# Paged latent decode woven into a feed-forward: six steps per half, three key buffers, scores in three bursts

## The chip, the cores and the metric

The kernel runs on one core of a Trainium2 chip. The metric is the device time of one execution in microseconds; three executions of the kernel before gave 1323.63, 1324.40 and 1324.49 us, median 1324.4. The engines are named as in the profile: PE is TensorE (PEld its weight loads), DVE VectorE, ACT ScalarE, POOL GpSimd, SP the queue that issues most DMAs.

## The reference

One layer of a hybrid decoder for 512 prompt tokens and a sample group of 8 sequences with 4 new tokens each, all in f32:

```python
h = x + 0.5 * post1(SwiGLU_1(pre1(x)))
u = pre_mix(h); z = u @ w_in
# HGRN2 group, 4 heads: gated linear recurrence over z
# MLA group, 4 heads: latent softmax attention, latent 256 + rotary key 64
h = h + post_mix(concat(o_hgrn, o_mla) @ w_out)
y = h + 0.5 * post2(SwiGLU_2(pre2(h)))
```

The prompt attends to itself. Each sample sequence attends to 4096 past positions too, whose latent rows (256) and rotary keys (64) lie in a pool of pages of 128 rows, found through `page_table`:

```python
s = einsum('bqhr,bsr->bhqs', ql, c_kv) + einsum('bqhd,bsd->bhqs', qr, k_rope)
p = softmax(where(k_pos <= q_pos, s * scale, -inf))
o_lat = einsum('bhqs,bsr->bqhr', p, c_kv)
```

## The kernel before, in words

**Tokens and products.** The 544 tokens are kept transposed (features on the partitions) in two halves: x = 0 holds 256 prompt tokens, x = 1 the other 256 and the 32 sample tokens (288 columns). Every large product is done in three passes of f32r: each operand is split into a rounded high piece and a remainder, and hi*hi, hi*lo and lo*hi are added up. A weight of 128 output columns (`weight`, L219) is loaded by SP into a raw buffer (`wraw`, 5 of them, L226), cast on ScalarE into `wh` (L237), and VectorE writes the remainder `wl` (L238). `wh` and `wl` have 2 buffers each, and 2 more while the second feed-forward's scope is open. `gemm` runs the 24 products of one weight and one half of the tokens.

**Stages.** First feed-forward for both halves (to 421 us), the mixer with the recurrence and the attention of the prompt (to 744 us), then the *decode stage*: the second feed-forward of half x = 0 (`gb`, an `ffn` generator, L297) is woven with the paged attention of the sample tokens. After it come the mixer's output projection for x = 1 with what is left of `gb` (`fill`, `FILL`), and the second feed-forward for x = 1.

**The feed-forward as a generator.** `ffn` walks the 22 column blocks of the inner width in four chunks of 6, 6, 5 and 5. For each block j it multiplies gate and up (48 products for one half of the tokens), forms the gated value and splits it into `hh` and `hl`, and yields. Behind each chunk it multiplies 8 down columns d (3 products for each inner block of the chunk) and yields after each. In all 54 such steps.

**The decode.** The 4096 x 8 past rows are 16 *halves* n (two for each sequence), each of two key blocks g of 128 partitions with 8 rows on each. A `Half` has these parts:
- `gather` (L1078): four indirect DMAs from POOL, two of latent rows (`craw`, 1 MB each, in six slots: three halves) and two of rotary keys (`rraw`, 4 buffers).
- `turn` (L1097): VectorE transposes both blocks in 32 x 32 squares into key buffers `kh` (`KHB` = 2 of them, so those of one half), six instructions at L1102 and L1103.
- `score` (L1106): 80 small f32 matmuls on 64 x 32 pieces of the array, two instructions each in the trace (160 records), for 10 key pieces j; after j = 9 VectorE takes the maxima.
- `peak` (L1126): TensorE turns the maxima, VectorE reduces them; `weigh` (L1135): two exponentials on ScalarE; `place` (L1140): VectorE transposes the weights into `pt`, then 16 small copies into `pbuf` (L1146), 8 on ScalarE and 8 on VectorE.
- `value` (L1148): 16 matmuls (32 records, L1154) of `pbuf` with the latent rows, which frees their slots; `gathered` (L1160) adds up every other half.

**The order around the change.** `decode` (L1168) runs three ticks for each half: in tick 0 the first five score pieces of half n - 2, a yield, then the other five, the values of n - 3 and the gather of n, a yield; in tick 1 the peak of n - 2 and the whole turn of n - 1, a yield; in tick 2 gathered(n - 3) and weigh(n - 2), a yield, place(n - 2). So four yields for a half. The driver below it (L1243 to L1254) takes 79 decode steps and 43 steps of `gb` in even proportion, and a step of a short generator for the new tokens with each decode step. Each engine works through its queue in order; the order in the queues follows the code, but the compiler's scheduler moves single instructions past one another.

Of the kernel before, what the change touches and what calls it, by code (L numbers as in the profile page):

```python
# [53 lines left out]
FILL = (4, (7, 8, 9), (1, 2, 3, 4), 4)  # L54
# [5 lines left out]
DRATE = 0.8  # L60
KHB = 2
# [42 lines left out]
def hybrid_step_kernel(  # L104
# [114 lines left out]
    def weight(srcs, kt, staged=False, home=None):  # L219
        if home is None and staged:  # L220
            pool, sfx, bufs = st, "x", STAG
        elif wx and wcnt[0] % (NW + WX) >= NW:
            pool, sfx, bufs = wx[0], "", WX
        else:
            pool, sfx, bufs = sb, "", NW
        w = mk([P, 8, P], F32, "wraw", 5, pool=sb)  # L226
        if home is None:
            wh = mk([P, 8, P], F32R, "wh" + sfx, bufs, pool=pool)
            wl = mk([P, 8, P], F32R, "wl" + sfx, bufs, pool=pool)
            wcnt[0] += not staged  # L230
# [25 lines left out]
    def gemm_q(wt, act_):  # L256
        wh, wl, kt = wt
        acc = ps("acc", "acc")
        n = act_[0].shape[-1]
        for k in range(kt):  # L260
            if k and k % 2 == 0:
                yield
            for i, (a, b) in enumerate(((wh, act_[0]), (wh, act_[1]), (wl, act_[0]))):
                nc.tensor.matmul(acc[:, :n], a[:, k], b[:, k], start=k + i == 0, stop=k == kt - 1 and i == 2)  # L264
        return acc[:, :n]

# [30 lines left out]
    def ffn(i, n_post, xs, u, nxt=None, mid=None, late=None, fin=None, pre=()):  # L297
# [5 lines left out]
        for c, (f0, nf) in enumerate(FCH[i]):  # L303
            hh = {x: mk([P, FCH[i][0][1], HS[x]], F32R, "hh" + "ab"[x], pool=pool) for x in xs}
            hl = {x: mk([P, FCH[i][0][1], HS[x]], F32R, "hl" + "ab"[x], pool=pool) for x in xs}
            for j in range(nf):
                f = f0 + j
                wg_ = (w0 or [weight([wcols(w_g[i], 0, KD, f * P)], KD)]).pop(0)
                ga = {x: gemm(wg_, u[x]) for x in xs}
# [3 lines left out]
                up = {x: gemm(wu_, u[x]) for x in xs}  # L313
# [16 lines left out]
            for grp in groups:  # L330
                wts = {d: pre.pop(0) if pre else weight([wcols(w_d[i], f0, nf, d * P)], nf, len(grp) > 1) for d in grp}
                for x in xs:
                    for d in grp:
                        acc = gemm(wts[d], (hh[x], hl[x]))
# [15 lines left out]
                yield  # L350
# [665 lines left out]
    gb = ffn(1, 5, (0,), u4, late=lambda: rstd_u(u4[0], 0), pre=seam)  # L1016
    next(gb)

    with scope("dec"):
# [48 lines left out]
        NS = 3 * NH2 + 11  # L1068
# [3 lines left out]
        class Half:  # L1072
# [24 lines left out]
            def turn(self):  # L1097
                self.kh = []
                for g in range(2):
                    kh = mk([P, ROWS, 10, 32], F32, "kh", KHB)  # L1100
                    for a in range(0, ROWS, 4):
                        nc.vector.transpose(kh[:, a : a + 4, :8].rearrange("p a j k -> p a (j k)"), self.craw[g][:, a : a + 4])  # L1102
                    nc.vector.transpose(kh[:, :, 8:].rearrange("p a j k -> p a (j k)"), self.rraw[g])  # L1103
                    self.kh.append(kh)
# [63 lines left out]
        def decode():  # L1168
            H = {}
            for t in range(NS):  # L1170
                n, r = divmod(t, 3)
# [4 lines left out]
                if n < NH2 and r == 0:  # L1176
                    H[n] = Half(n)
                if r == 0:
                    if at(2):
                        at(2).score(range(5))  # L1180
                    if n < 3 and at(0):
                        at(0).gather()
                    yield
                    if at(2):
                        at(2).score(range(5, 10))
                    if at(3):
                        at(3).value(H.get(n - 4))
                    if n >= 3 and at(0):
                        at(0).gather()
                    yield  # L1190
                elif r == 1:
                    if at(2):
                        at(2).peak()
                    if at(1):
                        at(1).turn()
                    yield
                else:
                    if at(3):
                        at(3).gathered()
                    if at(2):  # L1200
                        at(2).weigh()
                    yield
                    if at(2):
                        at(2).place()
# [39 lines left out]
        next(ga)  # L1244
        na, nb = NS + (NS + 2) // 3, int((22 + 32) * DRATE)
        ia, ib = 1, 0
        while ia < na:
            if ia * nb <= ib * na:
                next(ga, None)
                next(gn, None)  # L1250
                ia += 1
            else:
                next(gb, None)
# [165 lines left out]
```

## Time and profile before

| | us |
|---|---|
| median of three runs | 1324.4 |
| the profiled execution | 1323.85 |
| its span (first to last instruction) | 1322.1 |
| TensorE busy, granted clock | 1282.5, 0.995 |
| VectorE / ScalarE / GpSimd busy | 888.4 / 697.2 / 75.2 |

Busy time of TensorE counts a matmul from its start to a modelled end, and matmuls overlap in the pipeline; so its busy time is not useful time, and holes are read from the starts of neighbouring instructions. [...] "issue" as a releaser means that the profile shows nothing that the engine waited for.

### The profile page before, as it was taken

To read this page: it belongs to the slowest core of one execution; us is meant where nothing else is said; L and a number is where in the kernel's file an instruction comes from. 1 tells how busy PE (TensorE), PEld (TensorE's weight loads), DVE (VectorE), ACT (ScalarE), POOL (GpSimd) and SP (SyncE) were. 2 spreads that over 40 slices of the span, in tenths; PEclk is the share of its full clock that TensorE was granted. 3 is DMA by queue.
4 is the path that set the end of the run, shared out by engine and by line. 5 is a ranking of instruction groups with operands and counts; after the bars stand their busy time and mean duration, and the time that the engine had idled before them with its cause. 6 is when DMAs were issued, how large, how long until landed. Compare 5 with 4: busy or idle time off the path is not lost.

```text
span 1322.1 us, 30477 instructions
## 1 busy us (share of the span) xinstructions
PE 1282.5 (97%) x12696; PEld 1202.2 (91%) x12696; DVE 888.4 (67%) x1782; ACT 697.2 (53%) x1454; POOL 75.2 (6%) x79
## 2 busy tenths in 40 slices
PE   7999999999999999999999999989899999999997
PEld 7999999999999988889897887887788999999996
DVE  7553244434457787876867889989888868466664
ACT  6543344324456654444747665563455777554454
POOL 0000000000000000000000312313210000000000
PEclk9999999999999999999999999999899999999999
DMA  7323232333253323323222778968768645656551
GB/s 214 90 80 96 81 97 75 86 96 89 79 160 105 104 58 85 94 79 105 83 92 81 285 230 281 307 224 303 262 208 275 176 128 175 175 146 184 141 157 48
DMA packets 280552, 192.87 MB, mean 146 GB/s; under 512 B 12765, under 2 KB 271422, under 8 KB 275550
## 3 DMA queue, kind: packets, MB, share of 16 engines
q1 hardware_dynamic: 271968, 147.85, 38.8%
q0 software_dynamic: 7168, 41.95, 8.4%
q8 instruction: 100, 1.64, 0.5%
q10 hardware_dynamic: 1278, 1.12, 0.3%
q14 instruction: 38, 0.31, 0.1%
HBM read 181.22 MB, written 9.67 MB: 144 GB/s over the span
## 4 chain that ended last, share of the span: by engine, by line
PE 79%; DVE 11%; ACT 5%; issue 3%; DMA 2%; SPq 0%; DVEq 0%; ACTq 0%
PE acc L246 59%; PE acc L264 9%; DVE kh L1102 3%; DVE wl L238 2%; PE s L1115 2%; ACT wh L237 2%; PE s L919 1%; PE o L1154 1%; PE pa L658 1%; DMA wraw<-w_d 1%; PE zx L551 1%; ACT pbuf L1146 1%; DVE ssq L173 1%; PE pr L179 1%; DMA xt<-x_p 1%
## 5 line engine op out<-in xcount | busy, mean ns | idle before, releaser
L237 ACT CAST wh<-wraw 128x1024 fp32r<-128x1024 f32 (+3 forms) x255 | 248.2, 976 | 315.4 <-PE acc L246 276.6
L238 DVE TENSOR_TENSOR wl<-wraw,wh 128x1024 fp32r<-128x1024 f32 (+3 forms) x255 | 288.7, 1133 | 139.7 <-ACT wh L237 138.9
L246 PE MATMUL acc<-uhb,wh 128*128 128x288 f32 x768 | 227.9, 297 | 0.8 <-ACT uhb L195 0.8
L246 PE MATMUL acc<-ulb,wh 128*128 128x288 f32 x768 | 227.3, 296 | 0.0
L246 PE MATMUL acc<-uhb,wl 128*128 128x288 f32 x768 | 225.9, 295 | 1.2 <-DVE wl L238 1.2
L246 PE MATMUL acc<-uha,wh 128*128 128x256 f32 x768 | 220.3, 287 | 2.3 <-DVE sil L318 1.0
L246 PE MATMUL acc<-uha,wl 128*128 128x256 f32 x768 | 217.1, 284 | 1.3 <-DVE wl L238 1.2
L246 PE MATMUL acc<-ula,wh 128*128 128x256 f32 x768 | 217.1, 283 | 0.6 <-DVE ula L196 0.6
L246 PEld LDWEIGHTS acc<-uha,wh 128*128 128x128 f32 x768 | 145.5, 190 | 7.1 <-issue 3.3
L246 PEld LDWEIGHTS acc<-uha,wl 128*128 128x128 f32 x768 | 145.2, 190 | 2.3 <-DVE wl L238 2.3
L246 PEld LDWEIGHTS acc<-ula,wh 128*128 128x128 f32 x768 | 145.3, 189 | 1.1 <-DVE ula L196 1.0
L246 PEld LDWEIGHTS acc<-uhb,wl 128*128 128x128 f32 x768 | 144.5, 188 | 1.7 <-DVE wl L238 1.7
L246 PEld LDWEIGHTS acc<-uhb,wh 128*128 128x128 f32 x768 | 144.2, 188 | 1.6 <-ACT uhb L195 1.0
L246 PEld LDWEIGHTS acc<-ulb,wh 128*128 128x128 f32 x768 | 144.2, 188 | 0.1
L246 PE MATMUL acc<-hhb,wh 128*128 128x288 f32 x317 | 93.6, 297 | 0.9 <-ACT hhb L158 0.9
L246 PE MATMUL acc<-hlb,wh 128*128 128x288 f32 x317 | 94.0, 297 | 0.1
L246 PE MATMUL acc<-hhb,wl 128*128 128x288 f32 x317 | 93.0, 294 | 0.0
L246 PE MATMUL acc<-hha,wh 128*128 128x256 f32 x297 | 87.1, 293 | 1.4 <-ACT hha L158 1.4
L246 PE MATMUL acc<-hla,wh 128*128 128x256 f32 x297 | 84.4, 284 | 1.1 <-DVE hla L159 1.1
L246 PE MATMUL acc<-hha,wl 128*128 128x256 f32 x297 | 84.4, 284 | 0.3 <-DVE wl L238 0.2
L321 DVE TENSOR_TENSOR sil<-sil,acc 128x256 f32<-128x256 f32 (+1 forms) x88 | 38.2, 436 | 49.6 <-PE acc L246 47.7
L320 DVE TENSOR_TENSOR sil<-sil,sit 128x256 f32<-128x256 f32 (+1 forms) x88 | 38.5, 441 | 44.9 <-ACT sit L295 44.5
(476 smaller groups left out, 2765.7 us busy)
## 6 DMA issues: line engine op xcount, KB each, us to landing
wraw<-w_g SPq DMA_DIRECT2D x66, 512.0 KB, 4.3
wraw<-w_u SPq DMA_DIRECT2D x66, 512.0 KB, 4.0
wraw<-w_in SPq DMA_DIRECT2D x24, 512.0 KB, 4.0
wraw<-w_d SPq DMA_DIRECT2D x32, 384.0 KB, 4.3
wraw<-w_d SPq DMA_DIRECT2D x32, 320.0 KB, 3.3
wraw<-w_o SPq DMA_DIRECT2D x16, 512.0 KB, 4.1
wraw<-w_d SPq DMA_DIRECT2D x16, 448.0 KB, 3.7
wraw<-w_d SPq DMA_DIRECT2D x8, 512.0 KB, 4.0
```

The source lines that it names most:

```text
L173: (eng or nc.vector).tensor_tensor(acc, acc, q, op=ALU.add)
L179: nc.tensor.matmul(pr[:, :n], ones, acc, start=True, stop=True)
L237: nc.scalar.copy(wh[:, :kt], w[:, :kt])
L238: nc.vector.tensor_tensor(wl[:, :kt], w[:, :kt], f32(wh[:, :kt]), op=ALU.subtract)
L246: nc.tensor.matmul(out, a, b, start=n == 0, stop=n == last)
L264: nc.tensor.matmul(acc[:, :n], a[:, k], b[:, k], start=k + i == 0, stop=k == kt - 1 and i == 2)
L320: nc.vector.tensor_tensor(s, s, t, op=ALU.mult)
L321: nc.vector.tensor_tensor(s, s, up[x], op=ALU.mult)
L551: nc.tensor.matmul(z, w[a][:, k], U[1][b][:, k], start=k + n == 0, stop=k == KD - 1 and n == 2)
L658: nc.tensor.matmul(pa[es, c * 32 : (c + 1) * 32].rearrange("p (n m) -> p n m", m=m), kx[:, cs], up(qx[:, cs]), start=True, stop=True, skip ...
L1102: nc.vector.transpose(kh[:, a : a + 4, :8].rearrange("p a j k -> p a (j k)"), self.craw[g][:, a : a + 4])
L1115: nc.tensor.matmul(self.s[r][c * 32 : c * 32 + 32, :P], q[rs, j], kh, start=j == 0, stop=j == 9, skip_group_check=True)
```

## The change

- Scores in three bursts of 3, 3 and 4 key pieces, a yield after the first and the second. With the second burst the first key block of half n - 1 is turned (`turn(0)`); after the third burst the second block (`turn(1)`), then the values of n - 3 and the gather of n, a yield. Then peak, a yield; gathered and weigh, a yield; place runs together with the next first burst. Six yields ("steps") for a half, 114 in all. Key buffers `KHB` 2 to 3.
- The 16 placing copies are all on ScalarE.
- The feed-forward of x = 0 gets `fine=True`: gate and up products are cut in two pieces of 12 products with a yield between (`gemm_q` with step 4), and behind each chunk but the last the first two down columns are run together by `gemm_2`: all inner blocks but the last for both, a yield, then the last block for both. This makes 120 steps of what were 54.
- The driver takes one decode step, then `gb` steps in the proportion 100 to 114; the generator for the new tokens steps with every other decode step. `FILL[0]` goes from 4 to 13, since a step is now smaller: 100 steps end at the same inner block as 43 did.
- To make room, raw weight buffers go from 5 to 4 for the whole kernel, and the scratch for gather descriptors from 4096 to 2048 bytes.

```diff
-FILL = (4, (7, 8, 9), (1, 2, 3, 4), 4)
+FILL = (13, (7, 8, 9), (1, 2, 3, 4), 4)
-DRATE = 0.8
-KHB = 2
+NDEC = 100
+KHB = 3
...
-        w = mk([P, 8, P], F32, "wraw", 5, pool=sb)
+        w = mk([P, 8, P], F32, "wraw", 4, pool=sb)
...
-    def gemm_q(wt, act_):
+    def gemm_q(wt, act_, step=2):
...
-            if k and k % 2 == 0:
+            if k and k % step == 0:
                 yield
...
+    def gemm_2(wts, act_):
+        kt = wts[0][2]
+        n = act_[0].shape[-1]
+        accs = [ps("acc", "acc")[:, :n] for _ in wts]
+        for ks in (range(kt - 1), (kt - 1,)):
+            for (wh, wl, _), acc in zip(wts, accs):
+                for k in ks:
+                    for i, (a, b) in enumerate(((wh, act_[0]), (wh, act_[1]), (wl, act_[0]))):
+                        nc.tensor.matmul(acc, a[:, k], b[:, k], start=k + i == 0, stop=k == kt - 1 and i == 2)
+            if len(ks) > 1:
+                yield
+        return accs
...
-                ga = {x: gemm(wg_, u[x]) for x in xs}
+                ga, up = {}, {}
+                for x in xs:
+                    ga[x] = (yield from gemm_q(wg_, u[x], 4)) if fine else gemm(wg_, u[x])
+                if fine:
+                    yield
...
-                up = {x: gemm(wu_, u[x]) for x in xs}
+                for x in xs:
+                    up[x] = (yield from gemm_q(wu_, u[x], 4)) if fine else gemm(wu_, u[x])
...
+                if fine and not last and grp[0] == 0:
+                    accs = yield from gemm_2([weight([wcols(w_d[i], f0, nf, d * P)], nf) for d in (0, 1)], (hh[xs[0]], hl[xs[0]]))
+                elif fine and not last and grp[0] == 1:
+                    accs = accs[1:]
...
-            def turn(self):
-                self.kh = []
-                for g in range(2):
-                    kh = mk([P, ROWS, 10, 32], F32, "kh", KHB)
...
+            def turn(self, g):
+                if g == 0:
+                    self.kh = []
+                kh = mk([P, ROWS, 10, 32], F32, "kh", KHB)
...
-                        (nc.scalar.copy if g % 2 else nc.vector.tensor_copy)(self.p[g * 32 : g * 32 + 32, c // 2, c % 2 * 4 : c % 2 * 4 + 4, self.i * 16 : self.i * 16 + 16], src)
+                        nc.scalar.copy(self.p[g * 32 : g * 32 + 32, c // 2, c % 2 * 4 : c % 2 * 4 + 4, self.i * 16 : self.i * 16 + 16], src)
...
-            for t in range(NS):
-                n, r = divmod(t, 3)
+            for n in range(NH2 + 3):
...
-                if n < NH2 and r == 0:
+                if n < NH2:
                     H[n] = Half(n)
-                if r == 0:
+                for r, js in enumerate((range(3), range(3, 6), range(6, 10))):
                     if at(2):
-                        at(2).score(range(5))
-                    if n < 3 and at(0):
+                        at(2).score(js)
+                    if r == 0 and n < 3:
                         at(0).gather()
+                    if r == 1 and at(1):
+                        at(1).turn(0)
                     yield
...
+                if at(1):
+                    at(1).turn(1)
+                if at(3):
+                    at(3).value(H.get(n - 4))
+                if n >= 3 and at(0):
+                    at(0).gather()
+                yield
+                if at(2):
+                    at(2).peak()
+                yield
+                if at(3):
+                    at(3).gathered()
+                if at(2):
+                    at(2).weigh()
+                yield
+                if at(2):
+                    at(2).place()
...
-        na, nb = NS + (NS + 2) // 3, int((22 + 32) * DRATE)
-        ia, ib = 1, 0
-        while ia < na:
-            if ia * nb <= ib * na:
-                next(ga, None)
+        na, ib = 6 * (NH2 + 3), 0
+        for ia in range(na):
+            next(ga)
+            if ia % 2:
                 next(gn, None)
-                ia += 1
-            else:
-                next(gb, None)
+            while ib * na < (ia + 1) * NDEC:
+                next(gb)
                 ib += 1
...
-    nc = _bacc.Bacc("TRN2", target_bir_lowering=False, num_devices=1, dynamic_dma_scratch_size=4096)
+    nc = _bacc.Bacc("TRN2", target_bir_lowering=False, num_devices=1, dynamic_dma_scratch_size=2048)
```

## Rows read from the trace of the kernel before

**Rows 1.** The page: busy us of engines; DMA queue with packets, MB, share.

```profile
PE 1282.5 (97%) x12696; PEld 1202.2 (91%) x12696; DVE 888.4 (67%) x1782; ACT 697.2 (53%) x1454; POOL 75.2 (6%) x79
...
q8 instruction: 100, 1.64, 0.5%
```

**Rows 2.** The chain of waits in order of time (start, us, what), decode stage.

```profile
949.34 5.97 PE acc L246 x48
```

**Rows 3.** Busy time by stretch: stretch, its us, PE, PEld, DVE, ACT, POOL, clock, DMA.

```profile
764.00:1036.00 272.00, 256.50 (x4439) 220.92 (x4438) 238.63 (x531) 141.85 (x364) 59.66 (x55) 0.98 0.79 258
...
824.00:910.00 86.00, 81.36 (x1487) 69.86 (x1477) 78.88 (x171) 45.16 (x119) 25.03 (x23) 1.00 0.81 274
```

**Rows 4.** The chain of waits from 764 to 1036 us, shares by line.

```profile
by line: PE acc L246 35.6%; DVE kh L1102 13.5%; PE s L1115 9.5%; issue 7.5%; DVE wl L238 6.4%; PE o L1154 6.1%; ACT pbuf L1146 3.4%; ACT wh L237 3.3%; DVE kh L1103 2.3%; DVE pbuf L1146 1.5%; DVE mxd L1122 1.2%; DVE hla L159 0.9%; PE s L1128
```

**Rows 5.** TensorE's timeline: start, us to the last end, instructions, [idle before <- releaser].

```profile
901.09 0.28 PE L246 MATMUL acc<-hha,wl 128*128 128x256 f32 x1
901.30 1.37 PE L1115 MATMUL s<-kh,q 64*32 64x128 f32 x80
902.60 1.07 PE L1154 MATMUL o<-ha,pbuf 128*32 128x256 f32 x16
...
904.46 0.39 PE L246 MATMUL acc<-hha,wh 128*128 128x256 f32 x1
...
929.18 1.93 PE L1154 MATMUL o<-ulb,pbuf 128*32 128x256 f32 x16
...
941.29 2.26 PE L1115 MATMUL s<-kh,q 64*32 64x128 f32 x145
945.46 0.45 PE L1115 MATMUL s<-kh,q 64*32 64x128 f32 x15 [1.91 <-issue]
945.84 1.79 PE L1154 MATMUL o<-ha,pbuf 128*32 128x256 f32 x16
```

**Rows 6.** Busy time by stretch of 10 us, columns as in rows 3.

```profile
940.00:950.00 10.00, 8.09 (x209) 5.53 (x208) 8.65 (x20) 4.74 (x14) 0.94 (x1) 0.83 0.66 189
```

**Rows 7.** TensorE's waits, 764 to 1036 us: us in total, times, longest us.

```profile
PE s L1115 <- issue: 9.7, 6, 2.2
PE acc L246 <- ACT hha L158: 1.4, 2, 1.1
...
PE o L1154 <- issue: 1.2, 2, 1.0
PE acc L246 <- DVE hla L159: 1.1, 2, 0.6
...
PE o L1154 <- ACT pbuf L1146: 0.2, 1, 0.2
```

**Rows 8.** Groups by line, 744 to 1017 us: busy us, mean ns of one.

```profile
L1103 DVE STREAM_TRANSPOSE kh<-rraw 128x512 f32<-128x512 f32 x32 | 22.2, 693 | 0.0
L1102 DVE STREAM_TRANSPOSE kh<-ulb 128x1024 f32<-128x1024 f32 x12 | 14.8, 1232 | 0.3 <-PE s L1115 0.3
...
L1146 ACT COPY pbuf<-ulb 32x64 f32<-32x64 f32 x48 | 11.6, 242 | 1.4 <-DVE ulb L1142 0.5
...
L1146 DVE COPY pbuf<-ulb 32x64 f32<-32x64 f32 x48 | 9.2, 191 | 0.8
```

**Rows 9.** Gather on POOL, first transpose on VectorE (timelines); gathers into ha: us to landing.

```profile
903.97 0.94 POOL L1092 DMA_INDIRECT ha<-pool_c,idx  x1 [4.30 <-PE o L1154]
...
916.21 1.25 DVE L1102 STREAM_TRANSPOSE kh<-ha 128x1024 f32<-128x1024 f32 x1 [0.73 <-PE s L1115]
...
DMA to landing us min/median/max: 6.5/7.5/8.5
```

**Rows 10.** End of the first feed-forward: ScalarE's timeline; TensorE's waits, 32 to 421 us.

```profile
377.76 0.94 ACT L237 CAST whx<-wraw 128x896 fp32r<-128x896 f32 x1 [2.72 <-DMA wraw<-w_d]
...
PE acc L246 <- ACT hhb L158: 0.9, 1, 0.9
```

More of the change, by code (lines that the diff above doesn't have):

```diff
@@ L295, in sigmoid, with ffn @@
         nc.scalar.activation(out, out, AF.Exp, scale=-1.0)
-    def ffn(i, n_post, xs, u, nxt=None, mid=None, late=None, fin=None, pre=()):
+    def ffn(i, n_post, xs, u, nxt=None, mid=None, late=None, fin=None, pre=(), fine=False):
         pool = cur[-1]
@@ L330, in ffn @@
             for grp in groups:
-                wts = {d: pre.pop(0) if pre else weight([wcols(w_d[i], f0, nf, d * P)], nf, len(grp) > 1) for d in grp}
+                if fine and not last and grp[0] == 0:
+                    accs = yield from gemm_2([weight([wcols(w_d[i], f0, nf, d * P)], nf) for d in (0, 1)], (hh[xs[0]], hl[xs[0]]))
+                elif fine and not last and grp[0] == 1:
+                    accs = accs[1:]
+                else:
+                    accs = None
+                wts = None if accs else {d: pre.pop(0) if pre else weight([wcols(w_d[i], f0, nf, d * P)], nf, len(grp) > 1) for d in grp}
                 for x in xs:
                     for d in grp:
-                        acc = gemm(wts[d], (hh[x], hl[x]))
+                        acc = accs[0] if accs else gemm(wts[d], (hh[x], hl[x]))
                         if c == 0:
@@ L349, in ffn @@
                         next(ends[-1])
-                yield
+                if not accs or grp[0] == 0:
+                    yield
         if mid:
@@ L1015, in hybrid_step_kernel @@
     seam = []
-    gb = ffn(1, 5, (0,), u4, late=lambda: rstd_u(u4[0], 0), pre=seam)
+    gb = ffn(1, 5, (0,), u4, late=lambda: rstd_u(u4[0], 0), pre=seam, fine=True)
     next(gb)
@@ L1067, in hybrid_step_kernel @@
         NH2 = 2 * NB
-        NS = 3 * NH2 + 11
         PTG = {"ulb": 0, "uhb": -1, "ha": -1, "hb": 1, "mb": 0, "q0": -1}
@@ L1095, in gather @@
                     self.rraw.append(rraw)
-            def turn(self):
-                self.kh = []
-                for g in range(2):
-                    kh = mk([P, ROWS, 10, 32], F32, "kh", KHB)
[L1101 to L1104, printed above, removed]
+            def turn(self, g):
+                if g == 0:
+                    self.kh = []
+                kh = mk([P, ROWS, 10, 32], F32, "kh", KHB)
+                for a in range(0, ROWS, 4):
+                    nc.vector.transpose(kh[:, a : a + 4, :8].rearrange("p a j k -> p a (j k)"), self.craw[g][:, a : a + 4])
+                nc.vector.transpose(kh[:, :, 8:].rearrange("p a j k -> p a (j k)"), self.rraw[g])
+                self.kh.append(kh)
             def score(self, js):
@@ L1169, in decode @@
             H = {}
-            for t in range(NS):
-                n, r = divmod(t, 3)
+            for n in range(NH2 + 3):
                 def at(k):
                     return H.get(n - k)
-                if n < NH2 and r == 0:
+                if n < NH2:
                     H[n] = Half(n)
-                if r == 0:
+                for r, js in enumerate((range(3), range(3, 6), range(6, 10))):
                     if at(2):
-                        at(2).score(range(5))
-                    if n < 3 and at(0):
+                        at(2).score(js)
+                    if r == 0 and n < 3:
                         at(0).gather()
+                    if r == 1 and at(1):
+                        at(1).turn(0)
                     yield
[L1184 to L1196, printed above, removed]
-                else:
[L1198 to L1204, printed above, removed]
+                if at(1):
[12 more added lines that the diff above has]
+                    at(2).weigh()
+                yield
+                if at(2):
+                    at(2).place()
                 H.pop(n - 5, None)
@@ L1243, in hybrid_step_kernel @@
         ga, gn = decode(), decode_new()
-        next(ga)
-        na, nb = NS + (NS + 2) // 3, int((22 + 32) * DRATE)
-        ia, ib = 1, 0
-        while ia < na:
-            if ia * nb <= ib * na:
-                next(ga, None)
+        na, ib = 6 * (NH2 + 3), 0
+        for ia in range(na):
+            next(ga)
+            if ia % 2:
                 next(gn, None)
-                ia += 1
-            else:
-                next(gb, None)
+            while ib * na < (ia + 1) * NDEC:
+                next(gb)
                 ib += 1
```

## Prediction

> **What bounds the kernel now.** I read the page's busy table first: TensorE shows 97% of the span, VectorE 67% [rows 1]. Matmuls overlap, so that 97% is not 97% of useful work; the useful rate is 0.124 us for one 256-column product (48 in 5.97 us) [rows 2]. Next I cut the span into stages. The change is aimed at one of them, the decode stage, from 764 us to where the last prompt work that is woven into it ends at 1036 us: 272 us, TensorE 256.5 busy, VectorE 238.6 (88%), ScalarE 141.9 (52%), DMA share 0.79 [rows 3]. In its middle, 824 to 910 us, VectorE is busy 78.9 of 86.0 us (92%) [rows 3]. Then the chain of waits of that stage: TensorE's products, scores and values hold about half of it, VectorE 25.8% (kh 13.5 + 2.3, wl 6.4, pbuf 1.5, mxd 1.2, hla 0.9), "issue" 7.5%, ScalarE's pbuf and wh 6.7% [rows 4]. So no single engine bounds the stage: TensorE sets the pace with VectorE close behind.
>
> Last I went through TensorE's own queue for what a hole looks like. A burst of 80 score records takes 1.30 us (901.30 to 902.60), and the values behind it 1.86 us [rows 5]. [...] In all TensorE lost 9.7 us in 6 such waits ahead of scores and 1.2 in 2 ahead of values; its waits for the elementwise engines are small: 1.4 and 1.1 us for the last hidden pieces (hha, hla), 0.2 for pbuf [rows 7].
>
> **The change part by part.** The sum goes against the profiled execution's own 1323.85 us (span 1322.1 and 1.75 around it); that is 0.55 under the median of the three runs, 1324.4.
>
> *Three bursts (48, 48, 64 records) with prompt work between them.* The driver now takes 100 pieces over 114 decode steps, before 43 over 79, so nearly every burst has a piece of at least 12 products (1.5 us) behind it. The longest run of score records without a break falls from 160 to 64 (two bursts meet only where a step gets no piece, one in eight). The holes came behind 145 records, so I take 85% of the 10.9 us as gone: **-9.3** (bounds 0 and -10.9). The first 16 value records took 1.93 and 1.79 us at 929 and 946 us where 1.07 is usual [rows 5], 0.86 and 0.72 more, and the other 16 as much again: 2 x 1.58, **-3.1** (0 to -3.1) if the clock then holds. Against this, 16 more bursts: a burst starts 0.21 us after the product ahead of it instead of 0.12, and the first product behind one shows 0.39 us instead of 0.28 [rows 5], so 0.2 us each: **+3.2** (0 to +8, if the finer pieces cost as much again).
>
> *Dense half pieces.* At the end of each chunk two down products now run over all rows but the last, and only then need the last hidden piece. The waits for hha and hla go, 1.4 + 1.1 us [rows 7]: **-2.5** (0 to -2.5). Splitting gate and up into half products adds no instruction.
>
> *Placing copies all on ScalarE.* There are 16 halves with 8 copies on each engine. VectorE's cost 191 ns, 128 x 0.191 = 24.4 us of its 238.6 [rows 8]; ScalarE's cost 242 ns, so it gains 31.0 us and comes to 173 of 272 us, which fits. Of VectorE's time about a quarter lies on the chain, so 24.4 x 0.258: **-6.3** (bounds 0 and -24.4). Of ScalarE's, 6.7%: **+2.1**. The copies of a half now follow one another on one engine and end 8 x 0.242 = 1.9 us later; the values wait for them, but TensorE has four pieces and two and a half bursts in between, and the wait was 0.2 us in the whole stage [rows 7, 8]. Its upper bound is every half in full, 16 x 1.9 = 31 us.
>
> A moved copy costs 51 ns more on ScalarE than it did on VectorE [rows 8]. [...]
>
> *The second key block turned behind the scores, three key buffers.* VectorE does the same transposes, for a half 2 x (2 x 1.232 + 0.693) = 6.3 us [rows 8]; they are cut in two, and the first block no longer waits for the scores of the half before to free a buffer. What moves is the time that a gather has. The gather of a half is issued behind the values that free its buffers. Before, four prompt steps of 2.07 us (43 steps hold 1320 products, 163.7 us, over 79) and two bursts of 1.30 stood between it and the first transpose, 10.9 us; in the trace 12.2 (903.97 to 916.21) [rows 9]. After, it is four of 1.44 and two bursts of 0.78: 7.3 us. The first block needs 0.94 for the issue and 7.5 to land (6.5 to 8.5) [rows 9], so it comes 1.1 us late by TensorE's clock. VectorE idles 16 x 1.1 = 17.6 us, a quarter of it on the chain: **+4.5** (bounds 0, if VectorE lags that much anyway, and 16 x 2.1 = 34 us). Behind a waiting transpose stand, in VectorE's own queue, the weight remainders (wl) that TensorE's next pieces need; four weight buffers cover it as long as the wait is short.
>
> *One raw weight buffer less (5 to 4), half the scratch for gather descriptors.* In steady stretches ScalarE is never late for a raw weight. It is at the end of the first feed-forward, where a cast waited 2.72 us for its load and TensorE then 0.9 us for hhb behind it [rows 10]. With one buffer less such a load starts one release later, about one cast (0.9 us) on: **+1.0** (0 to +4, if all of the four waiting casts there pass it on). POOL shows no wait for space, so the smaller scratch is taken at nothing; should it hold fewer than the four gathers of a half, they come later and the rival of the late gather below gets worse.
>
> Work after the stage is the same: 13 small fill steps are the 4 large ones of before.
>
> Sum: -9.3 - 3.1 + 3.2 - 2.5 - 6.3 + 2.1 + 4.5 + 1.0 = **-10.4 us**, 1323.85 - 10.4 + 0.55 = **1314.0 us**.
>
> **The rivals.** *Forecast*: the holes behind long bursts go and half of the rest cancels, 1314, own range 1304 to 1321.
> *VectorE was the pace*: its 92% in the middle of the stage and the wl steps in the chain [rows 3, 4] speak for it, the small waits of TensorE for it [rows 7] against. Then the copies count in full: -24.4 - 3.1 + 3.2 + 1.0 = -23.3, 1301.
> *The holes only move*: TensorE must be supplied with the same number of instructions (instruction loads are 100 packets of 16.4 KB [rows 1]); if the supply and not the burst is short, the stalls appear ahead of the values or products, the dips of the clock too, and -2.5 + 3.2 is left: 1325, no change.
> *The gather is late* (slower): it decides as soon as landing exceeds 7.3 us by more than VectorE lags behind TensorE, and VectorE lags less once it has lost the copies. If the full 2.1 us a half falls on the path, +34 stands against VectorE's relief of 24.4, TensorE's holes lie under the wait and save nothing: +34 - 24.4 + 3.2 + 1.0 = +13.8, 1338. For it speaks the DMA share of 0.79, which a shorter stage raises; against it that no VectorE wait for a gather is among the waits now.
> *The change doesn't do what it says*: the queues show products inside bursts, so code order is not kept exactly; the third buffer might sit unused and only the lost weight buffer count, 1328.
>
> **How the numbers follow.** Chances: forecast 0.53, VectorE pace 0.16, holes move 0.13, gather late 0.14, nothing gained 0.04. The bound of no change is 0.2%, 2.6 us, about what a measurement of this kernel can tell: faster under 1321.8, slower over 1327.0. Faster 0.68 (forecast but for its upper edge, and VectorE pace), same 0.13, slower 0.19. The range 1300 to 1328 leaves out most of the late gather and the lower half of the VectorE case, under 0.2; the likeliest case alone is 1304 to 1321.
>
> **What would show it.** Right: the decode stage about 10 us shorter; "issue" ahead of scores under 2 us; granted clock near 1.00 from 920 us on; no wait for hha or hla; placing copies only on ScalarE, 256 of them. Wrong: VectorE's transposes wait for gathers (DMA as releaser); values wait for pbuf by more than 5 us; issue waits of some 10 us at other lines; or the stage is unchanged and TensorE waits for wl. If the time outside the stage moves by over 3 us, the weight buffer was mis-sized.

## The result, and the profile after

The changed kernel takes 1328.07 us (median of 20 runs, 1323.75 to 1334.45), the kernel before 1324.95 (20 runs beside it): ratio 1.0024, interval [1.0015, 1.0033]. It is slower, by 0.24% or 3.1 us; I had forecast 1314.0 and faster. The profiled execution is the longest of the twenty (1334.45; mean clock 0.988, the others 0.988 to 0.997), so its trace shows which waits came, and their sum is some 6 us too large.

The page's busy rows (us, share, instructions; answers to [rows 1]):

```profile
PE 1288.9 (97%) x12696; PEld 1206.4 (91%) x12696; DVE 864.0 (65%) x1654; ACT 726.5 (55%) x1582; POOL 73.2 (5%) x79
```

Moved as intended: 128 copies and 24.4 us from VectorE to ScalarE (+29.3). Up to 764 us the stages lie as before, to within 2 us. The 16 products that close the decode (L1261, the samples' output) begin at 1046.4 us, where those of the kernel before (L1240) began at 1036.3. Busy time of that stage and of four 10-us stretches in it, columns as in [rows 3]:

```profile
764.00:1046.00 282.00, 262.54 (x4434) 224.10 (x4433) 214.39 (x398) 170.51 (x488) 56.25 (x54) 0.96 0.77 248
...
770.00:780.00 10.00, 5.36 (x102) 4.38 (x101) 5.53 (x9) 3.62 (x6) 1.99 (x1) 0.81 0.38 106
780.00:790.00 10.00, 10.00 (x156) 8.92 (x162) 8.41 (x16) 3.64 (x9) 0.94 (x1) 0.85 0.82 235
810.00:820.00 10.00, 8.56 (x86) 6.42 (x86) 5.99 (x11) 3.53 (x9) 1.88 (x2) 0.66 0.24 58
900.00:910.00 10.00, 10.00 (x142) 9.24 (x142) 7.07 (x15) 7.49 (x26) 1.91 (x2) 0.71 0.72 255
```

VectorE is down to 76% of the stage (88% before), and the stage is longer all the same. The granted clock falls at three new places; over the stage it is 0.96, where [rows 3] has 0.98, which makes an estimate of at most 0.02 x 282, some 6 of the 10 us that the stage is longer. The waits of that stretch, TensorE's first, then VectorE's and ScalarE's (us in total, times, longest; [rows 7] is TensorE's list of before):

```profile
PE s L1152 <- DVE mxh L1148: 5.8, 4, 3.1
PE s L1139 <- issue: 5.5, 6, 3.0
PE acc L264 <- DVE wl L238: 4.6, 1, 4.6
...
DVE wl L238 <- ACT wh L237: 21.7, 12, 4.5
DVE sil L338 <- ACT sit L308: 13.6, 9, 4.5
DVE kh L1126 <- DMA ulb<-pool_c,idx: 5.5, 4, 2.7
DVE kh L1126 <- DMA mb<-pool_c,idx: 3.2, 3, 1.6
```

"issue" ahead of scores fell from 9.7 to 5.5 us and the waits for hha and hla are gone, but 5.8 us for mxh (the maxima ahead of the peak; 1.3 before) and 4.6 for wl have come. VectorE's 24 us of relief became waiting: for wh 21.7 us (8.3 before), for sit (ScalarE's part of the gated value) 13.6 (6.0), for gathers 8.7 (none): 29.7 us more. The chain of waits, 764 to 1046 us (answers to [rows 4]), says so too: a gather and a weight load stand in it, and kh has shrunk.

```profile
by line: PE acc L264 24.9%; PE acc L246 12.1%; PE s L1139 10.8%; issue 7.0%; PE o L1178 6.6%; DMA ulb<-pool_c,idx 5.7%; DVE kh L1126 4.8%; PE acc L275 4.5%; ACT pbuf L1170 3.7%; DMA wraw<-w_g 3.0%; DVE wl L238 2.8%; ACT wh L237 2.2%; PE s L
```

The three dips of the clock come with TensorE's three longest holes. From the timelines (start, us, what, [idle before <- releaser]), the first, on ScalarE and then TensorE:

```profile
773.68 1.04 ACT L237 CAST wh<-wraw 128x1024 fp32r<-128x1024 f32 x1 [6.07 <-DMA wraw<-w_g]
...
778.60 0.58 PE L264 MATMUL acc<-uha,wl 128*128 128x256 f32 x1 [4.64 <-DVE wl L238]
```

A raw gate weight lands late. In ScalarE's queue its cast and then sit stand behind it; VectorE waits 4.47 us for sit with the remainder wl behind that, and TensorE waits for wl. The second is a hole inside a last burst:

```profile
807.55 0.85 PE L1139 MATMUL s<-kh,q 64*32 64x128 f32 x38
811.44 1.08 PE L1139 MATMUL s<-kh,q 64*32 64x128 f32 x26 [3.04 <-issue]
```

The third, on ScalarE, VectorE and TensorE:

```profile
887.89 4.10 ACT L1170 COPY pbuf<-ulb 32x64 f32<-32x64 f32 x16
892.01 1.06 ACT L237 CAST wh<-wraw 128x1024 fp32r<-128x1024 f32 x1
...
893.10 1.22 DVE L238 TENSOR_TENSOR wl<-wraw,wh 128x1024 fp32r<-128x1024 f32 x1 [2.35 <-ACT wh L237]
...
897.98 0.45 DVE L1146 TENSOR_REDUCE mxd<-s 128x1 f32<-128x128 f32 x2
898.35 1.22 DVE L1126 STREAM_TRANSPOSE kh<-q 128x1024 f32<-128x1024 f32 x1
...
899.67 0.80 PE L1152 MATMUL s<-ident,mxh 128*128 128x128 f32 x2 [3.09 <-DVE mxh L1148]
```

The 16 copies stand in one block in ScalarE's queue; the cast behind them is late, VectorE waits for it in wl, the maxima behind that wl are late, and TensorE waits. Two transposes of 1.2 us stand on the way too (896.81 and 898.35), the second between the maxima and mxh. That is not new: the kernel before has one at this place in 15 of its 16 halves.

### The profile page after: what moved, and what is told of

Its sections match the earlier page's. It is cut to its first block, busy times and chain, and to the rows that moved or that the text cites. A ratio compares the mean times of both kernels' runs of the same rounds, so it can differ in the third digit from the quotient of the medians.

```text
span 1332.6 us, 30443 instructions
## 1 busy us (share of the span) xinstructions
PE 1288.9 (97%) x12696; PEld 1206.4 (91%) x12696; DVE 864.0 (65%) x1654; ACT 726.5 (55%) x1582; POOL 73.2 (5%) x79
## 4 chain that ended last, share of the span: by engine, by line
PE 79%; DVE 8%; ACT 5%; DMA 4%; issue 2%; SPq 0%; another core or an unknown queue 0%; DVEq 0%; ACTq 0%; POOLq 0%
PE acc L246 51%; PE acc L264 15%; PE s L1139 2%; DVE wl L238 2%; ACT wh L237 2%; PE o L1178 1%; PE s L944 1%; DMA ulb<-pool_c,idx 1%; DVE kh L1126 1%; DMA wraw<-w_g 1%; PE pa L683 1%; PE acc L275 1%; DMA wraw<-w_d 1%; ACT pbuf L1170 1%; PE zx L576 1%
## 5 line engine op out<-in xcount | busy, mean ns | idle before, releaser
L264 PE MATMUL acc<-uha,wh 128*128 128x256 f32 x528 | 159.9, 303 | 0.6 <-ACT uha L195 0.3
L264 PE MATMUL acc<-uha,wl 128*128 128x256 f32 x528 | 151.4, 288 | 4.9 <-DVE wl L238 4.9
L264 PE MATMUL acc<-ula,wh 128*128 128x256 f32 x528 | 151.8, 288 | 0.4 <-DVE ula L196 0.4
L246 PE MATMUL acc<-uha,wh 128*128 128x256 f32 x416 | 118.1, 284 | 1.0 <-DVE sil L336 1.0
L246 PE MATMUL acc<-uha,wl 128*128 128x256 f32 x416 | 117.5, 282 | 0.8 <-DVE wl L238 0.8
L246 PE MATMUL acc<-ula,wh 128*128 128x256 f32 x416 | 117.4, 282 | 0.2 <-DVE ula L196 0.2
L264 PEld LDWEIGHTS acc<-uha,wh 128*128 128x128 f32 x528 | 101.8, 193 | 13.6 <-issue 11.1
L264 PEld LDWEIGHTS acc<-uha,wl 128*128 128x128 f32 x528 | 102.1, 194 | 6.1 <-DVE wl L238 5.3
L264 PEld LDWEIGHTS acc<-ula,wh 128*128 128x128 f32 x528 | 102.2, 194 | 1.6 <-issue 0.8
L246 PEld LDWEIGHTS acc<-uha,wh 128*128 128x128 f32 x416 | 78.4, 188 | 1.5 <-DVE sil L336 1.2
L246 PEld LDWEIGHTS acc<-uha,wl 128*128 128x128 f32 x416 | 78.3, 188 | 1.4 <-DVE wl L238 1.4
```

Of the source, the lines that this page charges most:

```text
L246: nc.tensor.matmul(out, a, b, start=n == 0, stop=n == last)
```

## The experiments

Theories at the start: V, the copies' relief of VectorE is a gain (the prediction); D, late data cost the time (four raw weight buffers, gathers); S, switches between smaller pieces cost it. P, the block of copies on ScalarE ahead of the weight casts, came with f2_place; in the expectations of f1_raw4 to r1_coarse P still means that the values wait for the copies. The diffs give only the parts of the lines that change. Ratios are to the kernel before, run beside each on the same chip; E is the first of the 16 products of L1261 (or the same line elsewhere) in the trace.

| kernel | half pieces | three bursts | raw buffers | turned early | copies | median us | ratio [95%] | E |
|---|---|---|---|---|---|---|---|---|
| before | no | no | 5 | no | split | 1324 | 1 | 1036.3 |
| after | yes | yes | 4 | yes | ScalarE | 1328.07 | 1.0024 [1.0015, 1.0033] | 1046.4 |
| f1_raw4 | no | no | 4 | no | split | 1326.74 | 1.0017 [1.0000, 1.0033] | 1039.4 |
| f2_place | no | no | 5 | no | ScalarE | 1342.36 | 1.0153 [1.0131, 1.0175] | 1051.7 |
| f4_fine | yes | no | 5 | no | split | 1315.34 | 0.9934 [0.9921, 0.9947] | 1028.5 |
| f5_placefine | yes | no | 5 | no | ScalarE | 1331.13 | 1.0047 [1.0029, 1.0066] | 1042.3 |
| r1_coarse | no | yes | 4 | yes | ScalarE | 1346.77 | 1.0171 [1.0138, 1.0205] | 1063.7 |
| r4_both | yes | yes | 5 | no | split | 1321.65 | 0.9975 [0.9962, 0.9989] | 1033.3 |
| r5_raw4 | yes | yes | 4 | no | split | 1323.18 | 0.9986 [0.9975, 0.9998] | 1033.7 |
| r2_place | yes | yes | 4 | yes | split | 1328.04 | 1.0031 [1.0019, 1.0043] | 1045.7 |
| r3_turn | yes | yes | 5 | no | ScalarE | 1335.58 | 1.0087 [1.0071, 1.0103] | 1046.0 |

**f1_raw4.** Before, with one raw weight buffer less and half the scratch.

```diff
-"wraw", 5, pool=sb   dynamic_dma_scratch_size=4096
+"wraw", 4, pool=sb   dynamic_dma_scratch_size=2048
```

> The kernel before with 4 raw weight buffers instead of 5 and the smaller scratch, nothing else. Theory D (late data: with one raw buffer less, ScalarE waits for weight loads that queue behind gathers): slower than before by 3 to 8 us, and ScalarE's waits of wh for a load go from 2.8 us in the decode stage to over 8. Theory S (the finer weave costs TensorE) and theory P (the placing copies): within 1.5 us of before.

Measured 1326.74, ratio 1.0017 [1.0000, 1.0033], under D's range, with an interval that reaches down to no change. Its trace has the first of the three holes: ScalarE waits for the gate weight at 773 us. The others with four raw buffers (after, r1_coarse, r2_place, r5_raw4, a1_after99) have a wait of 5.3 to 7.7 us for w_g there; with five, none is over 2.5:

```profile
773.05 1.05 ACT L237 CAST wh<-wraw 128x1024 fp32r<-128x1024 f32 x1 [5.57 <-DMA wraw<-w_g]
```

**f2_place.** Before, with all placing copies on ScalarE.

```diff
-(nc.scalar.copy if g % 2 else nc.vector.tensor_copy)(self.p[...], src)
+nc.scalar.copy(self.p[...], src)
```

> The kernel before with all placing copies on ScalarE, nothing else. Theory P (the copies one after another end 1.9 us later and TensorE's values wait for them): slower by 4 to 15 us, waits of the values for pbuf over 3 us. Theory V (VectorE paces the stage, as a quarter of my sum had it): faster by 5 to 12 us. Theories D and S: within 2 us of before.

Measured 1342.36, ratio 1.0153 [1.0131, 1.0175]: 20 us slower. V falls, and so does P as it was expected here: the values wait 2.5 us for pbuf, and 20 us is over its range. ScalarE's, VectorE's and TensorE's timelines show one half of it:

```profile
822.60 4.24 ACT L1146 COPY pbuf<-mb 32x64 f32<-32x64 f32 x16 [0.73 <-DVE mb L1142]
826.86 0.37 ACT L336 COPY ma<-acc 128x256 f32<-128x256 f32 x1
827.26 1.05 ACT L237 CAST wh<-wraw 128x1024 fp32r<-128x1024 f32 x1
...
828.34 1.23 DVE L238 TENSOR_TENSOR wl<-wraw,wh 128x1024 fp32r<-128x1024 f32 x1 [4.67 <-ACT wh L237]
829.48 1.24 DVE L1102 STREAM_TRANSPOSE kh<-ha 128x1024 f32<-128x1024 f32 x1
830.64 0.45 DVE L1122 TENSOR_REDUCE mxd<-s 128x1 f32<-128x128 f32 x2
...
832.33 0.79 PE L1128 MATMUL s<-ident,mxh 128*128 128x128 f32 x2 [2.97 <-DVE mxh L1124]
```

Over the stage TensorE's wait for mxh rises from 1.3 to 11.0 us and VectorE's for wh from 8.3 to 34.5: 26 us of waiting for the 24 us that it gave up. Waits of the kernel before, then of f2_place:

```profile
DVE wl L238 <- ACT wh L237: 8.3, 17, 1.0
PE s L1128 <- DVE mxh L1124: 1.3, 5, 0.4
...
DVE wl L238 <- ACT wh L237: 34.5, 16, 4.7
PE s L1128 <- DVE mxh L1124: 11.0, 7, 3.0
```

The wait for mxh is the larger part of what is lost, not all of it: 9.7 us of the 15.4 by which E is later.

**f3_fine and f4_fine.** Before, with the half pieces alone: `gemm_q`, `gemm_2` and `ffn` of the change. f3_fine has one step fewer in the decode stage while the weights that are prepared ahead for the last chunk's down columns (`seam`) keep their count, so that down columns there are multiplied with other columns' weights. It computes another result, and only its time is read; f8_fine99 below has the same step fewer and the right columns.

```diff
-gb = ffn(1, 5, (0,), u4, late=..., pre=seam)
+gb = ffn(1, 5, (0,), u4, late=..., pre=seam, fine=True)
-FILL = (4, ...   nb = int((22 + 32) * DRATE)
+FILL = (13, ...  nb = 100 (f3_fine), 101 (f4_fine)
```

> The kernel before with the dense half pieces alone: gate and up products in two pieces, the first two down columns of a chunk run together, 100 steps in 79 decode steps; scores in two bursts, two key buffers, copies and raw buffers as before. Theory S: slower by 3 to 8 us, since each piece more costs TensorE a switch. My prediction's step: faster by 2 to 5 us, the waits for hha and hla gone. Theories D and P: faster by 0 to 3 us.

> The kernel before with the feed-forward's half pieces alone, 100 of them over the same 79 steps, all else as before (f3_fine gave 1309.6 with one step fewer in the decode stage, which took two down columns in another order). All theories: 1308 to 1312, issue ahead of scores 1 us where it was 9.7; it is the candidate that beats both kernels.

Measured 1309.56, ratio 0.9902 [0.9883, 0.9921], and 1315.34, 0.9934 [0.9921, 0.9947]: faster by 13 and 9 us with both bursts as they were, against S and by more than the 2 to 5 us of the prediction's step. "issue" ahead of scores is 1.0 us in f3_fine, but 6.3 in f4_fine, which is 3 us over its range:

```profile
PE s L1140 <- issue: 6.3, 9, 1.9
```

What the pieces do can be counted in the traces: in the stage of the kernel before, 7 stretches of 160 score records run through without a product between the two bursts; in f3_fine, f4_fine and f8_fine99 no stretch is longer than the 80 of one burst.

**r1_coarse.** After, with whole pieces.

```diff
-pre=seam, fine=True)   NDEC = 100   FILL = (13,
+pre=seam)              NDEC = 43    FILL = (4,
```

> The changed kernel with the feed-forward's steps as before (no half pieces, 43 steps over the 114 decode steps). Theory S: faster than the changed kernel by 3 us or more. If the half pieces are what cuts the score bursts apart: slower than the changed kernel by 5 to 10 us, with issue waits ahead of scores of 9 us or more. Theories D and P: within 3 us of the changed kernel.

Measured 1346.77, ratio 1.0171 [1.0138, 1.0205], 19.5 us over the changed kernel (0.0147 x 1324). S falls: the half pieces carry the change. The loss is over the 5 to 10 us expected, with 6.7 us of "issue" where 9 or more were; ten stretches of score records are 100 records or longer, up to 160, so three bursts by themselves don't keep the bursts apart.

**r2_place, r3_turn, r4_both.** After, with the copies split again; after, with both key blocks turned behind the peak, two key buffers and five raw ones; both together.

```diff
-nc.scalar.copy(self.p[...], src)                     (r2_place, r4_both)
+(nc.scalar.copy if g % 2 else nc.vector.tensor_copy)(self.p[...], src)
-                    if r == 1 and at(1): at(1).turn(0)  (r3_turn, r4_both)
-                if at(1): at(1).turn(1)
                 if at(2): at(2).peak()
+                if at(1): at(1).turn(0); at(1).turn(1)
-KHB = 3   "wraw", 4   scratch 2048
+KHB = 2   "wraw", 5   scratch 4096
```

> The changed kernel with the placing copies split again, 8 on VectorE and 8 on ScalarE. Theory P (the block of 16 copies on ScalarE holds back the weight casts queued behind it; VectorE then waits for wh before its wl, and its maxima behind that come late to TensorE; 18 us in the kernel before): the changed kernel's 1328 falls by 12 to 20, to 1308 to 1316, TensorE's wait at the peak for mxh from 5.8 us to under 2, and VectorE's wait for wh from 21.7 to under 12. Rival D (the loads: one raw weight buffer less, gathers in a block, the first transposes earlier): 1325 to 1330, as VectorE is loaded again and still waits for gathers and casts. Rival X (the finer pieces already cover what the block cost): 1322 to 1328.

> The changed kernel with both key blocks turned in one step behind the peak as before, two key buffers, five raw weight buffers and the larger scratch; three bursts, fine pieces and ScalarE's placing stay. Theory P: the loads are worth only the 2 to 3 us that the buffer alone cost, 1324 to 1328. Rival D: 1312 to 1320, and VectorE's kh waits for gathers (8.7 us) and ScalarE's 6 us wait for a raw weight at 768 us go.

> The kernel r3_turn with the placing copies split again as well: against the kernel before only the three bursts and the fine half pieces are left. If the parts add (P and the buffer): 1328 - 16 - 2.5 = about 1309, as the fine pieces alone (1309.6 in f3_fine), so that the three bursts add nothing. If three bursts do what the prediction said on top of fine pieces: under 1306. If their switches cost: 1313 to 1320.

r2_place (1328.04, ratio 1.0031) is over P's range and in those of D and X; r3_turn (1335.58, 1.0087) is over both; r4_both (1321.65, 0.9975) is just over that of costly switches. So the parts don't add. With late turning the move of the copies costs 14.8 us (r3_turn less r4_both), with early turning nothing clear of noise (after less r2_place: -0.9). Seen from the other side, turning early with the third key buffer and four raw buffers costs 7.4 us with split copies (r2_place less r4_both) and gains 8.3 with all of them on ScalarE (after less r3_turn). In r3_turn TensorE's wait for mxh explains less than in f2_place: 4.2 us (none in r4_both) of the 12.7 by which E is later; its waits ahead of scores for ScalarE's exponentials and for kh grow by some 4 us more, and about 3 more are lost to the clock, an estimate from the granted 0.992 over 1333.8 us here and 0.994 over 1320.9 in r4_both. In r2_place TensorE waits for mxh at the same place as in the changed kernel (3.81 us before 900.7), but there no cast is late; VectorE's first transpose waits for a gather, and eight copies, the weight remainders, more transposes and the maxima stand behind it:

```profile
889.48 1.25 DVE L1126 STREAM_TRANSPOSE kh<-mb 128x1024 f32<-128x1024 f32 x1 [2.72 <-DMA mb<-pool_c,idx]
...
891.80 1.22 DVE L1170 COPY pbuf<-ulb 32x64 f32<-32x64 f32 x6
...
899.05 0.45 DVE L1146 TENSOR_REDUCE mxd<-s 128x1 f32<-128x128 f32 x2
```

**f5_placefine.** f4_fine with f2_place's line.

> The kernel f4_fine (half pieces alone, 1315.3) with all 16 placing copies on ScalarE; bursts, turning and buffers as before. Theory P (the block of copies on ScalarE comes late to the weight casts behind it): most of the 18 us that the move cost in the kernel before comes back, 1326 to 1334, with TensorE's wait for mxh over 8 us and VectorE's wait for wh over 25. Rival X (the finer pieces cover the block): 1313 to 1319.

Measured 1331.13, ratio 1.0047 [1.0029, 1.0066], 15 us over f4_fine: P holds, with TensorE's wait for mxh 13.3 us and VectorE's for wh 32.3. The finer pieces don't cover the block.

**r5_raw4.** r4_both with f1_raw4's edit.

> The kernel r4_both (three bursts and half pieces, 1321.7) with four raw weight buffers and half the scratch; the key blocks still turned behind the peak, two key buffers. It splits the 6.4 us between r4_both and r2_place. Buffer: 1325 to 1328, with ScalarE's 5 to 6 us wait for the raw gate weight at 768 us and TensorE's 4 us behind it. Turning early: 1321 to 1323, no such wait.

Measured 1323.18, ratio 0.9986 [0.9975, 0.9998], between the two ranges: the wait for the gate weight comes (5.42 us), and the time is 1.5 us longer, which is not clear of noise; the other 6.0 up to r2_place belong to turning early with the third key buffer, where the copies are split.

**r6_two.** r4_both with two bursts.

```diff
-for r, js in enumerate((range(3), range(3, 6), range(6, 10))):
+for r, js in enumerate(((), range(5), range(5, 10))):
```

> The kernel r4_both with two bursts of 80 records instead of three, in the second and third of its six steps; the first has none. If the third burst's switches cost what the prediction priced (16 x 0.2): 1317 to 1319, against r4_both's 1321.7. If the six steps themselves cost (pieces spread thinner, so that steps come one behind the other too soon): 1321 to 1323. If three bursts save holes on top of the half pieces: 1324 to 1330, and issue ahead of scores over 6 us.

Measured 1320.06, ratio 0.9959 [0.9946, 0.9973], 2 us under r4_both, less than what alignment does (below), and between the first two ranges. Three bursts save no holes on top of the half pieces.

**r7_spread.** r3_turn with `place(c)` called once in each of four steps.

> The kernel r3_turn (all placing copies on ScalarE, key blocks turned behind the peak, 1335.6) with a half's 16 copies in four groups of four, one behind each of four steps, so that ScalarE's queue is never held for more than about 1 us; number and engine of the copies are the same. Theory P (a block in an in-order queue): 1316 to 1325, VectorE's wait for wh from 35.5 to under 15. Rival (31 us more of ScalarE's time is what costs): 1332 to 1338.

Measured 1336.16, ratio 1.0083 [1.0064, 1.0101]. The edit didn't reach the queue: the scheduler put the copies together again, in blocks of 12 to 16 for every half, so it doesn't test P, and that the time lies in the rival's range says nothing.

```profile
897.99 4.09 ACT L1170 COPY pbuf<-hb 32x64 f32<-32x64 f32 x16
```

**f6_vec, f9_pool, f10_sc_pool.** Before, with ScalarE's 8 copies on VectorE; with VectorE's 8 on GpSimd; with ScalarE's 8 on GpSimd.

```diff
-(nc.scalar.copy if g % 2 else nc.vector.tensor_copy)(...)
+nc.vector.tensor_copy(...)                                   (f6_vec)
+(nc.scalar.copy if g % 2 else nc.gpsimd.tensor_copy)(...)    (f9_pool)
+(nc.gpsimd.tensor_copy if g % 2 else nc.vector.tensor_copy)(...) (f10_sc_pool)
```

> The kernel before with the 8 placing copies of a half that stand on ScalarE put on VectorE as well (all 16 there): VectorE gains 128 x 0.191 = 24 us, ScalarE loses 31. Theory L (the weight casts run late in ScalarE's own queue, so its time counts more than VectorE's): 1315 to 1325, TensorE's wait for mxh no larger than before. Theory V (VectorE is next to the pace at 88%, the prediction's view): 1330 to 1345. Theory B (16 copies in one block hurt on whichever in-order queue they stand, as the maxima and the weight remainders stand in VectorE's): 1330 to 1345 too, but then f9_pool gives little.

> The kernel before with the 8 placing copies of VectorE put on GpSimd, the 8 of ScalarE left: VectorE's relief by itself, which the prediction priced at 6.3 us of 24.4. By the prediction: about 1318 (1310 to 1321), if GpSimd's copies come in time for the values. Theory L: VectorE's relief is worth under 3 us, 1321 to 1326. If GpSimd is slow at it (above 0.6 us a copy) the values wait for pbuf or the gathers come late: over 1330, and the trace shows which.

> The kernel before with the 8 placing copies of ScalarE put on GpSimd, the 8 of VectorE left: ScalarE's relief by itself, 128 x 0.242 = 31 us. By the prediction's 6.7% of the chain: 1322. Theory L: 1310 to 1319, VectorE's wait for wh under 8 us. GpSimd slow: as in f9_pool.

Measured 1333.39, ratio 1.0073 [1.0047, 1.0098]; 1340.36, 1.0128 [1.0106, 1.0151]; 1334.90, 1.0088 [1.0065, 1.0110]. L falls: all 16 on VectorE cost 10 us, with mxh at 6.7 us, in the range of V and of B alike. The two others tell little of a relief alone: a copy takes GpSimd under 0.4 us, below the 0.6 that was set for slow, and still the values wait for its copies (waits of f9_pool):

```profile
PE o L1154 <- POOL pbuf L1146: 13.1, 11, 3.1
```

In f9_pool TensorE's wait for mxh is down to 0.2 us, where the kernel before has 1.3, so VectorE is nearly off its path, but what the values wait is more than that gave. The split over ScalarE and VectorE is the fastest of the five placings tried.

**f8_fine99, a1_after99, f11_fine96.** One half piece moved from the decode stage to the fill behind it, in f4_fine and in the changed kernel; four moved in f4_fine.

```diff
-FILL = (13,   nb = 101 / NDEC = 100
+FILL = (14,   nb = 100 / NDEC = 99    (f8_fine99, a1_after99)
+FILL = (17,   nb = 97                 (f11_fine96)
```

> The kernel f4_fine (1315.3) with one half piece moved out of the decode stage into the fill behind it (99 and 14 for 100 and 13), as f3_fine had it (1309.6). If the 6 us between those two were the alignment of the pieces to the steps: 1307 to 1312. If f3_fine was fast for its other order of two columns: 1313 to 1317.

> The changed kernel with 99 half pieces in the decode stage and 14 in the fill behind it, for 100 and 13: the shift that took 5 us off the kernel with half pieces alone (1315.3 to 1310.2). If the changed kernel is slow for the parts of the change (block of copies, early turning, buffer): 1325 to 1331, as before the shift. If it only had an unlucky alignment: 1318 to 1323.

> The kernel f8_fine99 with three more half pieces moved into the fill (96 and 17). The size of what alignment alone does: between 1306 and 1318. No theory of the parts says more; below 1308 it would be the version to keep.

Measured 1310.17, ratio 0.9900 [0.9881, 0.9919]; 1330.30, 1.0046 [1.0029, 1.0063]; 1311.63, 0.9912 [0.9895, 0.9928]. How the pieces fall against the steps is worth 4.5 us in f4_fine and -2.9 in the changed kernel, so a difference of under 5 us between two variants isn't put down to a part. The one shift tried made the changed kernel slower, so nothing shows that it is slow for its alignment. f8_fine99 beats both kernels by 1.0 and 1.2%; no single wait of TensorE in its stage is over 1.7 us:

```profile
PE s L1153 <- DVE mxh L1149: 6.4, 7, 1.7
PE s L1140 <- issue: 1.7, 3, 0.8
PE s L1140 <- ACT q L1163: 0.9, 2, 0.7
```

## Why the prediction was wrong

A ladder of ratios leads from one kernel to the other (0.0001 is 0.13 us): half pieces -8.7 us (f4_fine), six steps with three bursts +5.4 (r4_both), raw buffer +1.5 (r5_raw4), turning early +6.0 (r2_place), copies -0.9 (after): +3.2 us, where the prediction's sum was -10.4. The raw buffer and the copies are within noise, and in another order the steps would get other sizes, since the parts don't add.

- **Holes and half pieces** (8.4 of the 13.6 us between the sum and the ladder): the step that failed first is "The holes came behind 145 records, so I take 85% of the 10.9 us as gone" (145 in [rows 5], 9.7 + 1.2 us in [rows 7]). It gave the holes to the three bursts (-9.3 - 3.1 + 3.2), with the finer pieces only to fall between them, and 2.5 us to the half pieces. The half pieces alone gave 8.7 us (13 in f8_fine99), with "issue" down to 6.3 us (1.7) and both bursts left whole: they put products between the two bursts, which three bursts with whole pieces (r1_coarse) don't. The third burst and the six steps gave nothing more and cost 5.4, at the edge of what alignment does. Together -3.3 us came of -11.7. The record count alone isn't the cause: five of the six holes ahead of scores in the kernel before come behind 111 to 155 records, but in the changed kernel the 3 us hole stands in a burst of 64, behind 38.
- **Placing copies**: the relief was counted by its share of the chain, -6.3, and ScalarE's gain by its own, +2.1. Both prices failed. The relief of 24.4 us came, and turned into waits, for casts above all. The share of the chain told nothing of what would stand behind a block of 4.1 us; the cover that the step named was for the values, and they indeed waited only 2.5 us in f2_place. By itself, or beside the half pieces, the move costs 20 and 15 us, within the upper bound of 31. In the change it is worth -0.9, where -4.2 was forecast.
- **Later gather, raw buffer**: +4.5 and +1.0 predicted, +6.0 and +1.5 on the ladder. The waits that were forecast came: VectorE waits for gathers (8.7 us, half of the 17.6 expected) and the DMA stands in the chain. That the sizes are near is luck: with all copies on ScalarE both together are worth -8.3. The place of the raw buffer's stall was not the end of the first feed-forward but the start of the decode stage, where the load was issued at 765 us and took 8.4.
- **Clock**: forecast near 1.00 from 920 us on, and 940 to 950 is at 1.00 (0.83 in [rows 6]). Stretches at half the clock came earlier, at the new holes (the changed kernel has 0.50 in each us from 777 to 783, 811 to 817 and 900 to 905, the kernel before from 929 to 932 and 947 to 949), and the sum had no term for them. r2_place's profiled execution, its slowest as is the changed kernel's, has the same three; its stage is at 0.96, that of r5_raw4 at 0.99, so an estimate of up to 0.03 x 282 = 8 of the 12 us between the two stages is clock.

Of the rivals, the late gather had the direction and part of the mechanism; its 13.8 us was too much. The number of the rival "doesn't do what it says", 1328, is met, but for another reason: every part did something. "The holes only move" (1325) named the supply of instructions, and the loads in the last section fit that; the new waits for mxh, wl and gathers it did not have.

Shown by runs: the half pieces' gain, that the third burst adds none to it, and the cost of moving the copies where the key blocks are turned late. Read from the traces only: the path block, cast, wl, maxima, TensorE, which covers some 4 to 10 us of that cost of 15 to 20; no run broke the block alone, since r7_spread's copies came together again. Left open: why the move costs 15 us with late turning and nothing with early turning. In r2_place and in the changed kernel a late gather and a late cast reach the same maxima at nearly the same time, which would make either free beside the other; that is argued. Turning early with five raw buffers wasn't tried; the change gave up the fifth to make room for the third key buffer.

The rows of f2_place at 822 to 832 us show the two queues in order: on ScalarE the cast starts at 827.26 us, behind 16 copies (4.24 us) and one more (0.37); VectorE idles 4.67 us ahead of wl, with a transpose and the maxima behind it, which then follow with no idle time.

## What to carry to other kernels

Before work moves from a busy engine to a half idle one, read what will stand behind it in the new queue and who waits for that: here a block of 16 copies in ScalarE's queue (4.24 us in f2_place) cost 15 to 20 us in the three kernels that turn their key blocks late, with ScalarE busy 52% of the stage in the kernel before ([rows 3]). Where a dense stream and bursts share TensorE, cut the stream before the bursts: here its pieces kept the bursts apart and gave 8.7 us, and cutting the bursts did neither (r1_coarse, r4_both). Time each part of a change by itself and on top of the others, and shift the interleave by one piece, before a few microseconds are credited to a part.

## What the hardware showed that I had not expected

The "issue" holes go with instruction loads. The kernel before has 35 of them (16.4 KB each) in the stage, one in 7.8 us; 7 of its 8 holes with "issue" end 2.25 to 2.55 us after one begins, a stretch of 0.3 us that chance would hit once in 26 times. The 3 us hole at 808.40 us in the changed kernel has one too, which begins 0.4 us into the hole and 2.6 us before its end (DMA queue, 808 to 810 us: packets, MB, share of 16 engines):

```profile
q8 instruction: 1, 0.02, 3.4%
```

In the decode stages of all twenty traces, 36 holes with "issue" last 1.2 us or more, and every one of them ends 2.2 to 2.6 us after a load begins; of the shorter ones many don't. That TensorE waits there for its next instructions fits this, and no run tested it. It would also say why the joined bursts suffer, by an estimate from [rows 1] that holds if these loads are TensorE's alone: 12696 matmuls and as many weight loads over 100 loads are 254 instructions a load, while 160 score records with their weight loads are 320, issued in 2.6 us.

GpSimd took 305 to 384 ns (f9_pool and f10_sc_pool) for the copy that takes ScalarE 242 and VectorE 191.
